# A transformer pair on one core: the order of units and loads in the first stage

## Chip, core and metric

The kernel runs on one core of one Trainium2 chip. The metric is device microseconds of one execution, the median of several. "PE" below is the matrix engine, "ACT" the scalar engine, "DVE" the vector engine; SP issues the loads. Each engine works through its own instructions in the order in which they are written.

## What is computed

Two transformer blocks in float32, 256 tokens of width 2048. The change lies in the front of the first block: a modulation vector from a conditioning vector, a normalised and modulated input for the tokens and for 256 context tokens, and the input projection.

```
mod_l = (jax.nn.silu(c) @ w_ada[l] + b_ada[l])[:, None, :]
mod_c = (jax.nn.silu(c_ctx) @ w_ada[l] + b_ada[l])[None, None, :]
...
h_l = modulate(rms_norm(x, g_mix_norm[l]), sh_a, sc_a)
h_c = modulate(rms_norm(xc, g_mix_norm[l]), csh_a, csc_a)
qa_l, kva_l, kr_l, cb_l, cc_l, ch_l = split_projection(h_l @ w_in[l])
qa_c, kva_c, kr_c, cb_c, cc_c, ch_c = split_projection(h_c @ w_in[l])
```

After it come the key/value and query projections (`wkvk`, `wkvv`, `wqb`), a convolution branch (`wconv`), attention, an output projection (`wout`), a feed-forward part and a second block. Those are not changed, except for where some chunks of `w_ada` are used.

## The kernel before, in words

Weights come from memory in chunks of at most 1 MiB (128 x 2048 floats) through one load queue. A chunk is used in "units". For most weights a unit is split: ACT casts it to a high part `wh` (a 768 or 1024 wide cast, L359) and DVE subtracts to get the low part `wl` (L360). Each product is then three matmuls (`wh` with `XH`, `wl` with `XH`, `wh` with `XL`), all recorded at line 411.

The first stage works over the 16 blocks of 128 channels in eight groups of two. Per group there are

- four "a" units: one 1 MiB chunk of `w_ada` each, not split, eight recorded matmuls `s<-raw,cn`. They accumulate the shift and scale rows of the group.
- then `gen_h`: a copy `arow` on ACT, four "row matmuls" `m<-cst,arow` that turn the rows into columns, small DVE steps (`SHG`), and for the tokens `X`, `XH`, `XL`, for the context `CX`, `cxh`, `cxl`. The context part needs `R0[1]`, the reciprocal root of the context's mean square.
- a "c" unit (18 matmuls), a "q" unit (24, the low-rank query input) and a "k" unit (36, key/value for tokens and context), which need the group's `XH` and `XL`, and k also `cxh` and `cxl`. A "C", "Q" or "K" chunk (0.75, 1 and 0.75 MiB) holds two such units.

The string `FIRST` is the order in which PE takes the units: the n-th "a" is `w_ada` chunk n, four per group, the n-th "c", "q" or "k" is that unit of group n. `LOADS` is the order of the loads. X comes ahead of both strings, the context CX ahead of the first K chunk. An "a" chunk has a ring of four buffers, C, Q and K have one buffer each, so a load waits on the queue until its buffer has been used, and the loads behind it wait too.

`gen_r0(0)` makes the mean square of X, `gen_r0(1)` that of CX: eight squares on ACT, sums on DVE, then matmuls with ones (`m<-sq,ones`): one for X, eight for CX, in pairs of the two token halves. The one for CX runs in one piece after unit c1.

The later chunks of `w_ada` are not used by PE: DVE multiplies each by the conditioning vector and sums (L349). The table `LATE` says behind which chunk of which weight how many of them stand; they go through the same ring of four buffers. The order of all 64 is fixed, and the table moves only the places. Casts are placed ahead of use by `look`, `AHEAD` = 4 units, with `NSPL` = 5 buffers for `wh` and `wl`.

`pump` lets pending pieces of `gen_h` and others go one step further; `kv` calls it after each third of a k unit, `unit_b` not at all.

Of the kernel before, what the change touches and what calls it, by code (L numbers as in the profile page):

```python
# [15 lines left out]
OP = mybir.AluOpType  # L16
# [19 lines left out]
AHEAD0 = 2  # L36
CXB = 3
AHEAD_N = ((0, 0), (0, 2), (1, 0))
FIRST = "aaaacq" "aaaac" "aaakakqc" + 5 * "aaaakqc" + "kq"
LOADS = "aaCaaQ" "aaaaK" + 3 * "aaaaCaaKaaQ"  # L40
NC0 = 2
KVY = 1
MG = (2, 2)
# [4 lines left out]
STAT0 = 0  # L48
ATT = (2, 4)
LATE = {  # L50
    "wconv": {2: 1, 3: 1, 5: 1, 7: 1, 8: 1, 9: 1, 10: 1, 11: 1, 12: 1, 13: 1, 14: 1, 15: 1, 16: 1, 17: 2, 20: 2,
              21: 2, 22: 1, 23: 1, 24: 3},
    "wkvk": {0: 1},
    "wkvv": {0: 1},
    "wqb": {0: 2, 1: 2, 2: 1},
    "wout": {0: 1, 1: 1, 5: 1, 2: 2, 7: 2, 9: 2, 11: 1, 14: 1},
    "wup": {**dict.fromkeys((0, 8, 1, 5, 9, 6), 1), **dict.fromkeys(range(14, 78, 4), 1)},
}
# [151 lines left out]
def _emit(tc, A, out, dbg=None):  # L210
    with ExitStack() as st:
        _body(st, tc, A, out, dbg or {})


def _body(st, tc, A, out, dbg):
    nc = tc.nc
    V, S, TE = nc.vector, nc.scalar, nc.tensor
# [14 lines left out]
    def plan_first():  # L232


        at, of = dict.fromkeys("aCQK", 0), {}
        for n in LOADS:
            i = at[n]
            at[n] += 1
            of[n.lower(), i] = len(chunks)
            if n == "a":  # L240
                chunks.append((A["wada0"][i // 4, i % 4], 2048, None))
            elif n == "Q":
                chunks.append((A["wqa"][i], 2048, "q"))
            else:
                chunks.append((A["wkc"][int(n == "C"), i], 1536, n.lower()))
        at = dict.fromkeys("aqck", 0)
        for n in FIRST:
            i = at[n]
            at[n] += 1
            if n == "a":  # L250
                u = Unit("ada0", of[n, i], (i // 4, i % 4 * 4, 4, 512, 0), True)
                u.native = True
            elif n == "q":
                u = Unit(n, of[n, i // 2], lay["wqa"][i // 2][i % 2], i % 2 == 1)
            else:
                u = Unit(n, of[n, i // 2], (0, 2 * i, 2, 384, 768 * (i % 2)), i % 2 == 1)
            events.append(u)
            first.append((n, i))
        return of
# [17 lines left out]
    of = plan_first()  # L277
# [23 lines left out]
    def pump():  # L301
        for ln in (EV, SIDE, MISC):
            ln.step()
# [13 lines left out]
    extra, pre = [None], {}  # L317

    def done_with(ci):
        raws.pop(ci)  # L320
        while nxt[0] < len(chunks) and room():
            issue()
# [49 lines left out]
    def look(n):  # L372

        seen, j = 0, ep[0]
        while j < len(events) and seen <= n:
            if not isinstance(events[j], tuple):
                seen += 2 if events[j].name in ("wkvk", "wkvv") else 1
            j += 1
        while sp[0] < j and (sp[0] < ep[0] + 1 or not hold(events[sp[0]])):
            split_next()  # L380

    def unit(name, g, n=None):
        while isinstance(events[ep[0]], tuple):
            ep[0] += 1
        u = events[ep[0]]
        mark(u, count[0])
        assert u.name == name and u.g == g, (u.name, u.g, name, g)
        look(ahead[0] if n is None else n)
        ep[0] += 1
        return u  # L390
# [19 lines left out]
    def mm(ps, l, r, start, stop, **kw):  # L410
        count[0] = TE.matmul(ps, l, r, start=start, stop=stop, skip_group_check=True, **kw)  # L411

    def mm3(ps, wh, wl, xh, xl, start, stop):
        mm(ps, wh, xh, start, False)
        mm(ps, wl, xh, False, False)
        mm(ps, wh, xl, False, stop)

    def unit_b(name, g, pst, xh, xl, starts=(0, 2)):

        u = unit(name, g)  # L420
        kt = spec[name][0]
        for n in range(u.w // P):
            for ki in range(u.nk):
                k = u.k0 + ki
                o = ki * u.w + n * P
                mm3(pst(n), u.wh[:, o:o + P], u.wl[:, o:o + P], xh(k, u), xl(k, u),
                    k == 0 and n in starts, k == kt - 1)
        return u.k0 + u.nk >= kt

    def group_b(name, g, xh, xl, hook=None, m=None):  # L430

        m = m or MR.now()
        i = 0
        while True:
            done = unit_b(name, g, lambda n: m.bank(n // 2)[:, n % 2 * T:(n % 2 + 1) * T], xh, xl)
            if hook:
                hook(i)
            i += 1
            if done:
                return m  # L440
            pump()
# [81 lines left out]
    ones = cp.tile([P, P], F32, name="ones")  # L523
# [12 lines left out]
    xh = lambda k, u=None: XH[:, k, :]  # L536
    xl = lambda k, u=None: XL[:, k, :]
# [21 lines left out]
    def rstd(*a):  # L559
        for _ in rstd_steps(*a):  # L560
            pass
# [8 lines left out]
    with tc.tile_pool(name="b0", bufs=1) as b0:  # L570
        extra[0] = b0
        CT = b0.tile([P, 2, KD], F32, name="CT")
        CX = b0.tile([P, KD, T], F32, name="CX")
# [3 lines left out]
        def load_tokens(dst, src):  # L577
            for h in range(4):
                nc.sync.dma_start(dst[:, 4 * h:4 * h + 4, :], A[src][:, 4 * h:4 * h + 4, :])
# [7 lines left out]
        ident = cst("ident")  # L587
        load_tokens(X, "xt")
        pre[of["a", 2]] = lambda: nc.sync.dma_start(VE, A["vecs"])
        pre[of["k", 0]] = lambda: load_tokens(CX, "ctxt")  # L590
        pre[n_first] = load_rest
        while room():
            issue()
# [15 lines left out]
        def gen_r0(w):  # L609

            src = (X, CX)[w]
            ps = m0.t[:, w, :T]
            acc = None
            for q in range(8):
                sq = b0.tile([P, 2, T], F32, name="sq0", tag="sq0", bufs=4)
                S.activation(sq, src[:, 2 * q:2 * q + 2, :], AF.Square)
                if acc is not None:
                    V.tensor_tensor(sq, sq, acc, OP.add)
                acc = sq
                if w and q % 2:  # L620
                    for j in range(2):
                        mm(ps, ones, sq[:, j], q + j == 1, q + j == 8)
                    acc = None
            if not w:
                V.tensor_tensor(acc[:, 0], acc[:, 0], acc[:, 1], OP.add)
                yield
                mm(ps, ones, acc[:, 0], True, True)
            rstd(R0[:, w, :], ps, 1.0 / D, EPS)
            r0_done.add(w)

# [36 lines left out]
        for c in range(4):  # L667
            b = qs[c % 2]
            for k in range(4):
                tr(b.t[:, k * P:(k + 1) * P], CF[:, 0, 4 * c + k:4 * c + k + 1].to_broadcast([P, P]))  # L670
            V.tensor_copy(CBC[:, 512 * c:512 * c + 512], b.t)
        r0 = gen_r0(0)
        next(r0)

        def ada(i):

            g, kc = i // 4, i % 4
            u = unit("ada0", g, 0 if g < 2 else None)
            w = raws[u.chunk]
            for j in range(4):  # L680
                mm(am.t[32 * j:32 * j + 32, :], cn[:, u.k0 + j, :], w[:, j * 512:(j + 1) * 512], kc == 0, kc == 3,
                   tile_position=(0, 32 * j))
            done_with(u.chunk)
            if i == 1:
                next(r0, None)
            if kc == 3:
                EV.add(gen_h(g))
            pump()
            if kc == 3:
                look(0)  # L690
# [3 lines left out]
        def kv():  # L694
            u = unit("k", 0)
            cxh, cxl = CXS[u.k0 // 2]
            for n in range(3):
                for ki in range(2):
                    k = u.k0 + ki
                    o = ki * 384 + n * P  # L700
                    for w, (h, l) in enumerate(((xh(k), xl(k)), (cxh[:, ki, :], cxl[:, ki, :]))):
                        mm3(kvb[n][:, w * T:(w + 1) * T], u.wh[:, o:o + P], u.wl[:, o:o + P],
                            h, l, k == 0 and w == 0, k == KD - 1)
                pump()

        c0 = lambda n: m1.t[:, 1, :T] if n == 2 else cm.t[:, n * T:(n + 1) * T]
        banks = {"q": lambda n: qs[n // 2].t[:, (n % 2) * T:(n % 2 + 1) * T], "c": c0}
        for n, i in first:
            if n == "a":
                ada(i)  # L710
                continue
            while i not in (CXS if n == "k" else XS):
                pump()
            if n == "k":
                kv()
            else:
                unit_b(n, 0, banks[n], xh, xl, (0, 2) if n == "q" else (0,))
                if n + str(i) == "c1":
                    for _ in gen_r0(1):
                        pass  # L720
                pump()
        ahead[0] = AHEAD
        dump("XH", XH.bitcast(F32))
# [14 lines left out]
    with tc.tile_pool(name="b1", bufs=1) as b1:  # L738
# [40 lines left out]
        with tc.tile_pool(name="b1n", bufs=1) as bn:  # L779
# [78 lines left out]
            for g in range(2):  # L858
                u = unit("wkvk", g)
# [9 lines left out]
            for g in range(2):  # L869
                u = unit("wkvv", g)  # L870
# [286 lines left out]
    with tc.tile_pool(name="b2", bufs=1) as b2:  # L1157

        acc = b2.tile([P, 1, 2, T], F32, name="acc2")
# [773 lines left out]
```

## Time and profile before

| | |
|---|---|
| median of 3 runs | 2199.33 us (2196.23 to 2201.58) |
| profiled execution | 2189.7 us |
| its span | 2187.9 us |
| PE busy | 2145.6 us, 98% of the span |
| DVE busy, ACT busy | 1492.4 us (68%), 1100.3 us (50%) |
| loads | 467.71 MB, 214 GB/s on average |

The profiled execution is one run; its own time stands 1.8 us above its span. Busy times overlap between engines. A matmul's recorded duration is longer than the step to the next one, so PE's work is better counted in matmuls per stretch. "PEclk" is the granted clock, 1.00 at 2.4 GHz and 0.50 at 1.2 GHz.

### The profile page before, as it was taken

To read this page: it belongs to the slowest core of one execution; us is meant where nothing else is said; L and a number is where in the kernel's file an instruction comes from. 1 tells how busy PE (TensorE), PEld (TensorE's weight loads), DVE (VectorE), ACT (ScalarE), POOL (GpSimd) and SP (SyncE) were. 2 spreads that over 40 slices of the span, in tenths; PEclk is the share of its full clock that TensorE was granted. 3 is DMA by queue.
4 is the path that set the end of the run, shared out by engine and by line. 5 is a ranking of instruction groups with operands and counts; after the bars stand their busy time and mean duration, and the time that the engine had idled before them with its cause. 6 is when DMAs were issued, how large, how long until landed. Compare 5 with 4: busy or idle time off the path is not lost.

```text
span 2187.9 us, 40079 instructions
## 1 busy us (share of the span) xinstructions
PE 2145.6 (98%) x17282; PEld 2061.5 (94%) x17286; DVE 1492.4 (68%) x1976; ACT 1100.3 (50%) x1500; POOL 0.2 (0%) x4
## 2 busy tenths in 40 slices
PE   6999999999999999999999999999999999999999
PEld 3788889989999999999999989999999999999999
DVE  4458878877876676767777679675666756646565
ACT  3344555445544444455656443445446546645363
POOL 0000000000000000000000000000000000000000
PEclk9999999999999999999999999999999999999999
DMA  9877878858666666645555545444555554445553
GB/s 383 323 286 268 288 244 321 341 219 302 219 231 244 225 239 230 228 162 206 185 188 175 194 154 190 141 152 156 196 174 190 182 191 148 142 173 194 179 175 114
DMA packets 68434, 467.71 MB, mean 214 GB/s; under 512 B 7840, under 2 KB 8352, under 8 KB 16544
## 3 DMA queue, kind: packets, MB, share of 16 engines
q1 hardware_dynamic: 68256, 465.14, 59.0%
q8 instruction: 135, 2.21, 0.4%
q14 instruction: 43, 0.35, 0.0%
HBM read 463.01 MB, written 2.10 MB: 213 GB/s over the span
## 4 chain that ended last, share of the span: by engine, by line
PE 92%; DVE 4%; DMA 3%; ACT 1%; issue 1%; SPq 0%; ACTq 0%; DVEq 0%
PE m L411 78%; PE s L411 13%; DMA rawx<-in_wqa 1%; DVE wl L360 1%; DMA raw<-in_wada 1%; PE s L408 1%; DVE raw L349 1%; ACT wh L359 0%; DMA raw<-in_wconv 0%; DMA X<-in_xt 0%; DVE rp L1306 0%; DVE rp L1307 0%; ACT arow L635 0%; DVE X L1165 0%; DVE rp L788 0%
## 5 line engine op out<-in xcount | busy, mean ns | idle before, releaser
L411 PE MATMUL m<-XH,wh 128*128 128x256 f32 x4032 | 1143.5, 284 | 8.6 <-ACT XH L1206 4.1
L360 DVE TENSOR_TENSOR wl<-raw,wh 128x1024 fp32r<-128x1024 f32 (+1 forms) x672 | 800.3, 1197 | 502.1 <-ACT wh L359 501.2
L411 PE MATMUL m<-XH,wl 128*128 128x256 f32 x4032 | 1132.2, 281 | 0.6 <-DVE wl L360 0.6
L411 PE MATMUL m<-XL,wh 128*128 128x256 f32 x4032 | 1132.2, 281 | 0.1
L359 ACT CAST wh<-raw 128x1024 fp32r<-128x1024 f32 (+1 forms) x672 | 686.7, 1028 | 667.9 <-PE m L411 592.9
L411 PEld LDWEIGHTS m<-XH,wh 128*128 128x128 f32 x4032 | 761.9, 189 | 25.5 <-issue 15.9
L411 PEld LDWEIGHTS m<-XH,wl 128*128 128x128 f32 x4032 | 761.8, 189 | 3.8 <-issue 2.2
L411 PEld LDWEIGHTS m<-XL,wh 128*128 128x128 f32 x4032 | 761.4, 189 | 0.5 <-DVE XL L1209 0.4
L411 PE MATMUL m<-ahl,wh 128*128 128x256 f32 x1376 | 245.0, 281 | 0.5 <-DVE uf L1234 0.5
L411 PEld LDWEIGHTS m<-ahl,wh 128*128 128x128 f32 x1376 | 211.4, 189 | 0.7 <-issue 0.7
L411 PE MATMUL m<-ahl,wl 128*128 128x256 f32 x688 | 193.1, 281 | 0.0
L349 DVE SCALAR_TENSOR_TENSOR raw<-raw,CBC 128x2048 f32<-128x2048 f32 x64 | 145.4, 2283 | 0.5 <-DMA raw<-in_wada 0.4
L411 PEld LDWEIGHTS m<-ahl,wl 128*128 128x128 f32 x688 | 129.7, 189 | 0.0
L411 PE MATMUL s<-XH,wh 128*128 128x256 f32 x416 | 118.0, 284 | 3.5 <-ACT XH L655 3.5
L411 PE MATMUL s<-XL,wh 128*128 128x256 f32 x416 | 117.9, 283 | 0.0
L411 PE MATMUL s<-XH,wl 128*128 128x256 f32 x416 | 117.7, 283 | 0.0
L364 ACT CAST ahl<-AC 128x512 fp32r<-128x512 f32 x88 | 53.8, 611 | 89.0 <-PE m L411 89.0
L365 DVE TENSOR_TENSOR ahl<-AC,ahl 128x512 fp32r<-128x512 f32 x88 | 59.6, 677 | 38.7 <-ACT ahl L364 38.7
L411 PEld LDWEIGHTS s<-XH,wh 128*128 128x128 f32 x416 | 79.4, 191 | 3.7 <-ACT XH L655 3.7
L411 PEld LDWEIGHTS s<-XH,wl 128*128 128x128 f32 x416 | 79.5, 191 | 0.0
L411 PEld LDWEIGHTS s<-XL,wh 128*128 128x128 f32 x416 | 79.4, 191 | 0.0
L360 DVE TENSOR_TENSOR wl<-rawx,wh 128x768 fp32r<-128x768 f32 (+1 forms) x24 | 24.9, 1046 | 61.6 <-ACT wh L359 61.6
(387 smaller groups left out, 1677.6 us busy)
## 6 DMA issues: line engine op xcount, KB each, us to landing
raw<-in_wada SPq DMA_DIRECT2D x96, 1024.0 KB, 6.7
raw<-in_wup SPq DMA_DIRECT2D x86, 1024.0 KB, 4.9
raw<-in_wdown SPq DMA_DIRECT2D x40, 1024.0 KB, 4.8
raw<-in_wpg SPq DMA_DIRECT2D x32, 1024.0 KB, 4.9
raw<-in_wconv SPq DMA_DIRECT2D x28, 768.0 KB, 6.1
raw<-in_wout SPq DMA_DIRECT2D x16, 1024.0 KB, 6.3
raw<-in_wqA SPq DMA_DIRECT2D x16, 1024.0 KB, 4.8
raw<-in_wgA SPq DMA_DIRECT2D x16, 1024.0 KB, 4.8
```

The costliest lines, as they stand in the source:

```text
L349: V.scalar_tensor_tensor(r, r, 1.0, CBC, op0=OP.mult, op1=OP.mult, accum_out=ADA[:, b:b + 1])
L359: S.copy(e.wh[:, :n], r)
L360: V.tensor_tensor(e.wl[:, :n], r, e.wh[:, :n].bitcast(F32), OP.subtract)
L364: S.copy(e.x[:, 0, :e.nk], a)
L365: V.tensor_tensor(e.x[:, 1, :e.nk], a, e.x[:, 0, :e.nk].bitcast(F32), OP.subtract)
L408: count[0] = TE.transpose(o, i, ident)
L411: count[0] = TE.matmul(ps, l, r, start=start, stop=stop, skip_group_check=True, **kw)
```

## The change

The order strings and the late table change, q units let pending work go on after each quarter, and the mean square of CX is summed on DVE and takes one matmul.

```diff
-FIRST = "aaaacq" "aaaac" "aaakakqc" + 5 * "aaaakqc" + "kq"
-LOADS = "aaCaaQ" "aaaaK" + 3 * "aaaaCaaKaaQ"
+FIRST = "aaaac" "aaaaqc" "aaaaqck" + 5 * "aaaakqc" + "kkq"
+LOADS = "aaCaa" "Qaaaa" "aaaaCK" + 2 * "aaaaQaaKaaC" + "aaaaQK"
...
-    "wconv": {2: 1, 3: 1, 5: 1, 7: 1, 8: 1, 9: 1, 10: 1, 11: 1, 12: 1, 13: 1, 14: 1, 15: 1, 16: 1, 17: 2, 20: 2,
+    "wconv": {2: 1, 3: 1, 5: 1, 7: 1, 8: 1, 9: 1, 10: 1, 11: 1, 12: 1, 13: 1, 14: 1, 15: 1, 16: 1, 17: 2, 18: 1, 19: 1, 20: 2,
...
-    "wqb": {0: 2, 1: 2, 2: 1},
+    "wqb": {0: 1, 1: 1, 2: 1},
...
-    def unit_b(name, g, pst, xh, xl, starts=(0, 2)):
+    def unit_b(name, g, pst, xh, xl, starts=(0, 2), tick=None):
...
+            if tick:
+                tick()
...
-        pre[of["k", 0]] = lambda: load_tokens(CX, "ctxt")
+        pre[of["a", 8]] = lambda: load_tokens(CX, "ctxt")
...
-                if w and q % 2:
-                    for j in range(2):
-                        mm(ps, ones, sq[:, j], q + j == 1, q + j == 8)
-                    acc = None
-            if not w:
-                V.tensor_tensor(acc[:, 0], acc[:, 0], acc[:, 1], OP.add)
-                yield
-                mm(ps, ones, acc[:, 0], True, True)
+            V.tensor_tensor(acc[:, 0], acc[:, 0], acc[:, 1], OP.add)
+            yield
+            mm(ps, ones, acc[:, 0], True, True)
...
-        r0 = gen_r0(0)
-        next(r0)
+        sums = [gen_r0(w) for w in range(2)]
+        next(sums[0])
...
-            u = unit("ada0", g, 0 if g < 2 else None)
+            u = unit("ada0", g, 0 if g < 1 else 2 if g < 3 or kc < 3 else 1)
...
-            if i == 1:
-                next(r0, None)
+            if i in (1, 11):
+                next(sums[i > 1], None)
...
-                unit_b(n, 0, banks[n], xh, xl, (0, 2) if n == "q" else (0,))
+                unit_b(n, 0, banks[n], xh, xl, (0, 2) if n == "q" else (0,), pump if n == "q" else None)
                 if n + str(i) == "c1":
-                    for _ in gen_r0(1):
-                        pass
+                    next(sums[1])
```

Three places of the new order follow. In the rows, a tile's number tells buffers apart.

PE from unit c0 (into `s_120` and `m_116`) to unit c1, first before. `s_117` and `s_118` take the q unit, `s_119` the four a units.

```order
L411 MATMUL m_116<-XL_69,wh_206 128x256
L411 MATMUL s_117<-XH_68,wh_224 128x256
...
L411 MATMUL s_118<-XL_69,wh_224 128x256
L411 MATMUL s_119<-raw_170,cn_106 32x512 x4
L411 MATMUL s_119<-raw_176,cn_106 32x512 x4
L411 MATMUL s_119<-raw_190,cn_106 32x512 x4
L411 MATMUL s_119<-raw_196,cn_106 32x512 x4
L411 MATMUL m_116<-cst0_87,arow_294 128x2 x4
L411 MATMUL s_120<-XH_68,wh_296 128x256
```

The same stretch of PE after the change, again from the end of c0 to the start of c1.

```order
L411 MATMUL m_116<-XL_69,wh_200 128x256
L411 MATMUL s_119<-raw_170,cn_106 32x512 x4
L411 MATMUL s_119<-raw_176,cn_106 32x512 x4
L411 MATMUL s_119<-raw_190,cn_106 32x512 x4
L411 MATMUL s_119<-raw_196,cn_106 32x512 x4
L411 MATMUL s_117<-XH_68,wh_252 128x256
...
L411 MATMUL m_116<-cst0_87,arow_276 128x2 x4
...
L411 MATMUL s_118<-XL_69,wh_252 128x256
L411 MATMUL s_120<-XH_68,wh_262 128x256
```

Unit q0 has moved from ahead of the four a units to behind them, and the row matmuls stand inside it, after its first six matmuls. In group 2 q1 stands in the same way around the row matmuls.

ACT from the last square of the context to the copy `arow` of group 2 and a little on, before. `R0` is the reciprocal root; casts from `rawx_202` are k0 and k1, from `rawx_104` q1, from `rawx_300` c2.

```order
L616 ACTIVATE sq0_357<-CX_83 128x512
L549 ACTIVATE R0_114<-rsm_362 128x256
L550 ACTIVATE R0_114<-R0_114 128x256
L655 ACTIVATE cxh_216<-CX_83,SHG_71 128x256 x2
L655 ACTIVATE cxh_308<-CX_83,SHG_71 128x256 x2
L359 CAST wh_387<-rawx_202 128x768
L359 CAST wh_401<-rawx_202 128x768
L359 CAST wh_445<-rawx_104 128x1024
L635 COPY arow_457<-s_119 128x512
L359 CAST wh_459<-rawx_300 128x768
```

The same stretch of ACT after the change; here `rawx_272` is c2 and `rawx_274` k0.

```order
L618 ACTIVATE sq0_354<-CX_83 128x512
L359 CAST wh_370<-rawx_104 128x1024
L359 CAST wh_380<-rawx_272 128x768
L551 ACTIVATE R0_114<-rsm_393 128x256
L552 ACTIVATE R0_114<-R0_114 128x256
L652 ACTIVATE cxh_210<-CX_83,SHG_71 128x256 x2
L652 ACTIVATE cxh_290<-CX_83,SHG_71 128x256 x2
L632 COPY arow_408<-s_119 128x512
L359 CAST wh_410<-rawx_274 128x768
```

The casts of q1 and c2 have moved ahead of the root, those of k0 behind `arow`. In both orders `arow` of group 2 stands behind the root and the four `cxh` copies.

The queue of loads around `wqb`, the difference of the two orders.

```order
 L340 DMA raw<-in_wqb 128x2048
-L340 DMA raw<-in_wada 128x2048 x2
+L340 DMA raw<-in_wada 128x2048
 L340 DMA raw<-in_wqb 128x2048
-L340 DMA raw<-in_wada 128x2048 x2
+L340 DMA raw<-in_wada 128x2048
 L340 DMA raw<-in_wqb 128x2048
```

One late chunk stands behind each of the first two `wqb` chunks where there were two; the two removed ones stand behind `wconv` 18 and 19.

## Rows read from the trace of the kernel before

**Rows 1.** The page, share of the span and chain by engine

```profile
PE 2145.6 (98%) x17282; PEld 2061.5 (94%) x17286; DVE 1492.4 (68%) x1976; ACT 1100.3 (50%) x1500; POOL 0.2 (0%) x4
...
PE 92%; DVE 4%; DMA 3%; ACT 1%; issue 1%; SPq 0%; ACTq 0%; DVEq 0%
```

**Rows 2.** Stretches of 10 us: busy per engine (instructions), PEclk, DMA share, GB/s

```profile
30.00:40.00 10.00, 9.36 (x72) 6.52 (x70) 1.22 (x1) 0.70 (x3) 0.00 (x0) 1.00 1.02 417
...
110.00:120.00 10.00, 8.61 (x73) 8.41 (x72) 8.01 (x14) 5.76 (x9) 0.00 (x0) 1.00 0.91 381
...
210.00:220.00 10.00, 7.30 (x41) 7.10 (x40) 9.13 (x12) 5.45 (x7) 0.00 (x0) 0.67 0.99 366
```

**Rows 3.** Timeline of PE, 35 to 65 us: start, duration, instruction, idle before and releaser

```profile
35.72 3.64 PE L411 MATMUL s<-raw,cn 128*32 128x512 f32 x32
...
43.18 0.58 PE L411 MATMUL s<-XH,wh 128*128 128x256 f32 x1 [2.01 <-ACT XH L655]
...
46.22 0.29 PE L411 MATMUL m<-XH,wl 128*128 128x256 f32 x1
...
57.05 0.58 PE L411 MATMUL m<-XH,wh 128*128 128x256 f32 x1 [3.06 <-ACT wh L359]
...
63.30 0.28 PE L411 MATMUL m<-XH,wh 128*128 128x256 f32 x1
...
64.58 0.28 PE L411 MATMUL m<-cxl,wh 128*128 128x256 f32 x1
```

**Rows 4.** Timeline of ACT, 35 to 320 us

```profile
39.48 0.58 ACT L635 COPY arow<-s 128x512 f32<-128x512 f32 x1 [9.30 <-PE s L411]
...
54.56 1.70 ACT L655 ACTIVATE cxh<-CX,SHG 128x256 fp32r<-128x256 f32 x4 [1.93 <-DVE CX L653]
...
79.79 0.59 ACT L635 COPY arow<-s 128x512 f32<-128x512 f32 x1 [5.43 <-PE s L411]
...
93.64 0.59 ACT L635 COPY arow<-s 128x512 f32<-128x512 f32 x1 [6.17 <-PE s L411]
...
110.24 1.04 ACT L359 CAST wh<-rawx 128x1024 fp32r<-128x1024 f32 x1 [6.61 <-DMA rawx<-in_wqa]
...
140.87 0.58 ACT L635 COPY arow<-s 128x512 f32<-128x512 f32 x1
...
211.28 1.99 ACT L359 CAST wh<-raw 128x1024 fp32r<-128x1024 f32 x2 [8.53 <-DMA raw<-in_wqb]
...
318.09 0.83 ACT L359 CAST wh<-raw 128x768 fp32r<-128x768 f32 x1 [2.19 <-PE m L411]
```

**Rows 5.** Timeline of PE, 110 to 215 us

```profile
111.82 1.05 PE L411 MATMUL m<-cst,arow 128*128 128x2 f32 x8 [1.39 <-ACT arow L635]
...
214.24 0.58 PE L411 MATMUL m<-QAH,wh 128*128 128x256 f32 x1 [2.70 <-ACT QR L888]
```

**Rows 6.** Timeline of the load queue at a8 to a11

```profile
36.85 2.90 SPq L340 DMA_DIRECT2D raw<-in_wada  x4
```

**Rows 7.** Loads issued at 27.0, 204.6 and 307.1 us: size, time to landing

```profile
CX<-in_ctxt SPq DMA_DIRECT2D x1, 512.0 KB, 14.0
...
raw<-in_wqb SPq DMA_DIRECT2D x1, 1024.0 KB, 6.6
...
raw<-in_wconv SPq DMA_DIRECT2D x1, 768.0 KB, 4.3
```

**Rows 8.** Timeline of DVE, 50 to 205 us

```profile
51.31 0.42 DVE L543 TENSOR_SCALAR rsm<-m 128x256 f32<-128x256 f32 x1 [1.22 <-PE m L411]
...
157.66 0.69 DVE L729 COPY X<-s 128x512 f32<-128x512 f32 x1 [0.75 <-PE s L411]
...
198.95 1.23 DVE L360 TENSOR_TENSOR wl<-raw,wh 128x1024 fp32r<-128x1024 f32 x1 [0.69 <-ACT wh L359]
...
202.30 2.29 DVE L349 SCALAR_TENSOR_TENSOR raw<-raw,CBC 128x2048 f32<-128x2048 f32 x1
```

**Rows 9.** One stretch of 1 us: PE busy (matmuls), PEclk, DMA share, GB/s

```profile
219.00:220.00 1.00, 1.00 (x7) 0.50 0.99 420
```

## The prediction

> **What bounds the kernel now.** Read the page first: the matrix engine PE is busy for 98% of the span and holds 92% of the chain that ended last [rows 1]. So a change can pay only where PE stands idle or runs at its lower clock. The stretches of 10 us show where that is. At full speed PE can issue about 86 matmuls in 10 us (one in 0.1165 us, below). From 30 to 40 us it issues 72, although the DMA share is 1.02 at 417 GB/s: the loads set the pace. From 110 to 120 us it issues 73 with the clock at 1.00, and from 210 to 220 us 41 with a mean clock of 0.67 [rows 2]. The change touches both places.
>
> Prices for the first stage come from the timeline of PE [rows 3]. At the full clock 64.58 - 63.30 = 1.28 us hold eleven steps, 0.1165 us each. A c unit (18 matmuls) costs 2.10 us, a q unit (24) 2.80, a k unit (36) 4.19. Four a units back to back take 3.64 us, 0.91 each. A unit's first matmul after a wait lasts 0.58 us instead of 0.28: the lower of the clock's two levels, 1.2 instead of 2.4 GHz. One such start at 43.18 is at full speed again by 46.22, the one at 57.05 only at 63.30; so 3.0 to 6.2 us at half speed, a loss of 1.5 to 3.1 us.
>
> The stage is paced by the copy arow, one per group, which starts when that group's four a units are done [rows 4]. From 79.79 to 93.64 a period is 13.85 us; the sum 4.19 + 2.80 + 2.10 + 3.64 plus row matmuls of 1.05 [rows 5] is 13.8, so PE alone sets that one. The next three periods take 47.23 together, 15.7 each: the cast of a q unit waited 6.61 us for its load (until 110.24) in front of an arow on ACT's in-order queue, and PE idled 1.39 us before the row matmuls at 111.82; there are two such places, in groups 5 and 7 [rows 4, 5].
>
> **The change, part by part.**
>
> *q0 behind group 1.* Before, q0's 2.80 us stand between c0 and a4, and after a7 PE has nothing until XH is ready: arow 39.48, c1 at 43.18 after 2.01 idle, then 3 us at the low clock [rows 3, 4]. After, c0 ends where it does, a4 to a7 run 2.8 us earlier (arow 36.7), and the 3.70 us from arow to XH are covered by q0 with the four row matmuls inside it, 2.80 + 1.05 = 3.85. c1 then runs at full speed from about 40.4 to 42.5 instead of 43.18 to 46.8. Those 4.3 us cannot be cashed at once, because loads come next.
>
> *k0, k1 behind group 2 and the loads so ordered.* The last part of CX lands at 27.0 + 14.0 = 41.0 [rows 7]. Before, a8 was issued at 36.85, after a4's matmuls had freed its buffer, and it came behind chunk K0 [rows 6]. After, a8 to a11 follow CX directly: at 417 GB/s 1 MiB takes 2.5 us, so a11 lands at 50.9, and C1 (0.75 MiB) at 52.8. PE waits for these loads in either kernel, so c1's earlier end is hidden here.
>
> *One sum matmul instead of eight, and what ACT does around it.* The order below shows what is not in the diff: in group 2 arow stands on ACT behind the CX reciprocal root and four cxh copies. The sum matmul comes after a11, and the root on DVE behind c2's low half, which needs C1: 52.8, a cast of 0.83 (as at 318.09, [rows 4]) and about 1 us on DVE, 54.6. From that DVE step to the end of the four cxh copies it took 51.31 to 54.56 + 1.70 = 56.26, that is 4.95 us [rows 4, 8]. So arow of group 2 starts at 59.5 and the row matmuls end at 61.2. PE has only six matmuls of q1 before them and idles about 4 us from 55. This wait takes the place of the old one (57.05, after 3.06 idle). Then follow q1's rest 2.10, c2 2.10, k0 4.19, a12 to a15 3.64: 12.0 us, and 2.2 for the low clock (middle of 1.5 and 3.1). arow of group 3 is at 75.4 instead of 79.79: 4.4 us earlier, but with one k unit (k1, 4.19 us) not yet done. Up to here the change gains 0.2 us.
>
> *From group 3 to the end of the stage.* Before, 79.79 to the last copy of the q banks at 157.66 is 77.87 us [rows 4, 8]. After, k1's 4.19 is added; the casts of q units now stand behind arow, and each Q chunk is issued ahead of the next group's a loads, so the two holes of 1.4 should go: 77.87 + 4.19 - 2.8 = 79.3. The end comes at 75.4 + 79.3 = 154.7: 3.0 us earlier. Bounds: if PE alone sets all four periods, 4 x 13.85 = 55.4 instead of 61.08 - 2.8 = 58.3, and with the smaller clock loss it is 6.6 earlier; if the holes stay and the clock loss is the larger, 0.9 later. I take 3.0, since chunks K1 and K2 still lie between a loads of groups 4 and 6.
>
> *Two 1 MiB ada chunks moved from behind wqb to behind wconv 18 and 19.* wqb's third chunk reuses the buffer of the chunk four places before it. Before, that is an ada chunk which DVE finishes at 202.30 + 2.29 = 204.6; the load, issued then, lands 6.6 us later at 211.2 [rows 7, 8]; ACT waited 8.53 us for it, PE idled 2.70 until 214.24 and was still at 0.50 at 219 to 220 us [rows 4, 5, 9]. After, the place four before is wqb's first chunk, whose second low half ends at 198.95 + 1.23 = 200.2 [rows 8], so the load can land at about 205 and its two casts end near 207; DVE also has two products of 2.29 us fewer ahead of it. PE has work to 211.5, so the hole closes: 2.7 us idle and half of some 6.2 us at the low clock, 5.8 in all. Bounds 0 and 5.8. In their new place the two products cost DVE 2 x 2.29 and the queue 2 x 2.5 us. wconv 20's load took 4.3 us [rows 7], and the first cast of its stretch, at 318.09, had waited 2.19 us for PE, that is for a buffer [rows 4]: casts run four units ahead, 4 x 2.1 = 8 us. I cost it at nothing; without that cover it would be a hole like wqb's, 5.8 us.
>
> **Sum.** 3.0 + 5.8 = 8.8 us earlier. The profiled execution took 2189.7 us (span 2187.9), so 2180.9; the three timed runs have a median of 2199.33, 9.6 above it, and the same difference gives 2190.5.
>
> **The rivals.** *First stage as before, only wqb closes.* The holes before arow go over into late a loads. For it: a DMA share of 0.91 between 110 and 120 us, near its limit [rows 2]. Then 5.8 earlier, 2193.5. *wqb's hole stays* because DVE's split is late by another way: 3.0 earlier, 2196.3. Against it: 4.6 us of DVE work are gone from in front of it. *Both better*: PE alone sets the periods, 12.4 earlier, 2186.9. *The clock.* In this trace the low clock follows the pauses of PE before c1, k0 and wqb's third chunk (2.0 to 3.1 us), but not the pause of 1.39 us, whose ten microseconds stay at 1.00 [rows 2, 3, 5]. If load waits of groups 4 to 7 each grew past that, four starts at 1.5 to 3.1 us would cost about 9: 2199.5, no change.
> The Trainium skill ("TensorE: Matmul & The Clock Gate", section "HAM oscillation — how this bites in real kernels") describes just this, matmul bursts between DMA waits that each start at the low rate, and it speaks against an order that lets PE run ahead of its loads. By that rule group 2 pays, and the trace shows it for two pauses; no row shows it for groups 4 to 7.
>
> *Slower: the moved chunks starve wconv.* wconv 19, 20 and 21 would each come behind one or two more ada chunks in a ring of four buffers. If each became late as wqb was, three holes of 5.8 are 17.4 us, net 8.6 slower: 2207.9. It decides when wconv 20 lands later than 8 us after 318, its cast time plus the lead; before, it landed at about 311.4 (4.3 us after its issue at 307.1, [rows 7]), and two MiB more put it near 317. So it is unlikely.
>
> **How the numbers follow.** Forecast (both parts, 6 to 12 us) 0.60; only wqb 0.15; only the first stage 0.08; better than 12 us 0.05; clock, no change 0.06; slower 0.06. A measurement of this kernel can tell 0.2%, 4.4 us. Faster: 0.60 + 0.05 + most of the 0.15 and a little of the 0.08 = 0.79; same 0.14; slower 0.07. The range takes in the bounds of the two main terms, 2185 to 2198, and leaves out the no-change and slower cases and the far end of the better one.
>
> **What would show it.** Right: arow of group 1 near 36.7 with c1 entered at the full clock; a11's load at 51; arow of group 2 near 59.5 behind four cxh copies with PE idle some 4 us; arow of group 3 near 75; the last q copy near 154.7; no ACT wait for wqb over 3 us, and a clock of 1.00 in the ten microseconds around its third chunk; casts in the wconv stretch waiting for PE, not for loads. Wrong: arow of group 2 after 62, periods above 15 us from group 3 on, or a new DMA wait of ACT at wconv 19 to 21 with PE idle behind it.

## The result, and the profile after

| | before | after |
|---|---|---|
| median of 4 runs each | 2200.45 us (2196.23 to 2202.02) | 2185.34 us (2183.76 to 2186.54) |
| ratio | | 0.9946, 95% interval 0.9925 to 0.9967 |
| profiled execution | 2189.70 us | 2186.54 us |
| arow of groups 1, 2, 3, 7 start at | 39.48, 65.93, 79.79, 140.87 | 37.13, 59.20, 75.53, 131.88 |
| last q copy starts at | 157.66 | 153.63 |
| last QN copy (end of the `wqb` units) starts at | 222.89 | 212.98 |

By the ratio the change is 0.54% faster, 11.9 us of 2200; the ratio is not the quotient of the two medians, which stand 15.1 us apart. The forecast was 2190.5 with a range of 2185 to 2198: the time lies at the range's lower end, 0.3 us inside it. The page of the changed kernel, share of the span and chain by engine, beside [rows 1]:

```profile
PE 2147.1 (98%) x17268; PEld 2061.7 (94%) x17272; DVE 1494.4 (68%) x1980; ACT 1101.9 (50%) x1500; POOL 0.2 (0%) x4
...
PE 94%; DVE 2%; DMA 2%; ACT 1%; issue 0%; SPq 0%; ACTq 0%; DVEq 0%
```

The whole kernel looks the same; what moved is seen in stretches of 10 us, columns as in [rows 2]:

```profile
30.00:40.00 10.00, 10.00 (x69) 6.31 (x69) 2.69 (x6) 1.03 (x3) 0.00 (x0) 0.78 1.02 418
50.00:60.00 10.00, 4.69 (x21) 2.42 (x18) 4.24 (x9) 4.07 (x9) 0.00 (x0) 0.67 1.02 425
60.00:70.00 10.00, 10.00 (x66) 10.00 (x67) 7.19 (x16) 3.05 (x6) 0.00 (x0) 0.75 0.48 199
...
110.00:120.00 10.00, 10.00 (x88) 7.23 (x87) 2.90 (x6) 3.85 (x6) 0.00 (x0) 1.00 1.01 401
200.00:210.00 10.00, 10.00 (x88) 10.00 (x88) 9.97 (x13) 5.94 (x7) 0.00 (x0) 1.00 0.95 338
210.00:220.00 10.00, 10.00 (x70) 8.00 (x69) 9.82 (x13) 3.60 (x5) 0.00 (x0) 1.00 0.59 214
```

Both places of [rows 2] are full: 88 matmuls instead of 73 from 110 to 120 us, and PE never idle at a clock of 1.00 from 200 to 220 us. The third chunk of `wqb` is now cast at 201.19, so it is the stretch from 200 to 210 us, with 88 matmuls, that stands for the one with 41 before. The worst stretch left is 50 to 60 us: PE is busy for 4.69 of 10 us, with the loads at 425 GB/s. The timeline of ACT shows what paces it, beside [rows 4]:

```profile
37.13 0.59 ACT L632 COPY arow<-s 128x512 f32<-128x512 f32 x1 [6.90 <-PE s L411]
...
52.61 0.83 ACT L359 CAST wh<-rawx 128x768 fp32r<-128x768 f32 x1 [6.16 <-DMA rawx<-in_wkc]
54.80 0.42 ACT L551 ACTIVATE R<-rsm 128x256 f32<-128x256 f32 x1 [1.36 <-DVE rsm L545]
...
57.59 1.70 ACT L652 ACTIVATE cxh<-CX,SHG 128x256 fp32r<-128x256 f32 x4 [1.93 <-DVE CX L650]
59.20 0.56 ACT L632 COPY arow<-s 128x512 f32<-128x512 f32 x1
...
75.53 0.59 ACT L632 COPY arow<-s 128x512 f32<-128x512 f32 x1 [8.13 <-PE s L411]
...
89.61 0.59 ACT L632 COPY arow<-s 128x512 f32<-128x512 f32 x1 [6.09 <-PE s L411]
...
131.88 0.59 ACT L632 COPY arow<-s 128x512 f32<-128x512 f32 x1 [6.10 <-PE s L411]
...
201.19 2.01 ACT L359 CAST wh<-raw 128x1024 fp32r<-128x1024 f32 x2 [2.36 <-DMA raw<-in_wqb]
...
212.98 1.02 ACT L884 COPY QN<-m 128x1024 f32<-128x1024 f32 x1 [1.97 <-PE m L411]
```

ACT waits for chunk C1 until 52.61; the root, the `cxh` copies and `arow` follow one behind the other, the last with no idle time of ACT before it. From group 3 on every `arow` waits for PE alone and the periods are 14.1 us ((131.88 - 75.53) / 4 = 14.09). The wait for `wqb` is 2.36 instead of 8.53 us. PE in group 2, beside [rows 3]:

```profile
50.76 1.94 PE L411 MATMUL s<-raw,cn 128*32 128x512 f32 x8 [0.54 <-DMA raw<-in_wada]
52.62 1.22 PE L411 MATMUL m<-sq,ones 128*128 128x256 f32 x2
...
54.71 0.33 PE L411 MATMUL s<-XL,wh 128*128 128x256 f32 x1
59.82 1.87 PE L411 MATMUL m<-cst,arow 128*128 128x2 f32 x8 [4.77 <-ACT arow L632]
...
64.68 0.41 PE L411 MATMUL s<-XL,wh 128*128 128x256 f32 x1
...
65.09 0.28 PE L411 MATMUL s<-XH,wl 128*128 128x256 f32 x1
```

PE stands still for 4.77 us before the row matmuls; the matmuls after it come 0.21 us apart, the lower of the two clock levels, until 64.9. DVE, beside [rows 8], the root's first step and the end of the stage:

```profile
54.35 0.42 DVE L545 TENSOR_SCALAR rsm<-m 128x256 f32<-128x256 f32 x1
...
153.63 0.69 DVE L725 COPY X<-s 128x512 f32<-128x512 f32 x1 [0.72 <-PE s L411]
```

### The profile page after: what moved, and what is told of

It reads as the page before. It is cut to its first block, busy times and chain, and to the rows that moved or that the text cites. A ratio compares the mean times of both kernels' runs of the same rounds, so it can differ in the third digit from the quotient of the medians.

```text
span 2184.8 us, 40059 instructions
## 1 busy us (share of the span) xinstructions
PE 2147.1 (98%) x17268; PEld 2061.7 (94%) x17272; DVE 1494.4 (68%) x1980; ACT 1101.9 (50%) x1500; POOL 0.2 (0%) x4
## 4 chain that ended last, share of the span: by engine, by line
PE 94%; DVE 2%; DMA 2%; ACT 1%; issue 0%; SPq 0%; ACTq 0%; DVEq 0%
PE m L411 80%; PE s L411 14%; DVE wl L360 1%; DMA raw<-in_wada 1%; DMA rawx<-in_wkc 1%; PE s L408 1%; ACT wh L359 0%; DMA X<-in_xt 0%; DVE rp L1302 0%; DVE rp L1303 0%; DVE raw L349 0%; DVE X L1161 0%; ACT cxh L652 0%; DVE uf L1229 0%; DVE uf L1230 0%
```

## The experiments

The theory is the prediction's, in two parts: the first stage and `wqb`. Rivals: that the new order itself changes how closely PE's matmuls follow, since the traces differ in that, and that single steps are worth something else. All kernels with their marks (start in us of the copy `arow` of group 2, of the last q copy and of the last QN copy; matmuls from 500 to 550 us; ratio to the kernel before, on the same chip; e1 to e4 ran on one chip, e5 to e8 on a second, e9 to e12 on a third):

| kernel | arow 2 | q copy | QN copy | matmuls | ratio (95% interval) |
|---|---|---|---|---|---|
| before, shown ahead | 65.93 | 157.66 | 222.89 | 428 | |
| after | 59.20 | 153.63 | 212.98 | 424 | 0.9946 (0.9925 to 0.9967) |
| e1_before_again | 67.88 | 161.11 | 224.21 | 423 | 0.9996 (0.9981 to 1.001) |
| e2_late_only | 67.96 | 160.94 | 220.21 | 428 | 0.9971 (0.9957 to 0.9984) |
| e3_first_stage_only | 59.51 | 154.50 | 217.44 | 424 | 0.9978 (0.9965 to 0.9991) |
| e4_sum_after_a9 | 55.05 | 150.45 | 209.72 | 424 | 0.9931 (0.9913 to 0.9949) |
| e5_no_tick | 58.93 | 155.51 | 214.78 | 423 | 0.9955 (0.9941 to 0.997) |
| e6_q0_back | 58.94 | 153.37 | 212.64 | 424 | 0.9961 (0.9945 to 0.9976) |
| e7_eight_sums | 61.70 | 156.02 | 215.28 | 428 | 0.9967 (0.9954 to 0.998) |
| e8_early_root | 53.79 | 147.82 | 207.09 | 429 | 0.9934 (0.9914 to 0.9953) |
| e9_wconv_doubled | 59.84 | 155.13 | 214.38 | 424 | 0.995 (0.993 to 0.9969) |
| e10_k0_load_first | 61.28 | 155.83 | 215.09 | 424 | 0.9965 (0.9949 to 0.9982) |
| e11_after_again | 59.11 | 154.58 | 213.84 | 423 | 0.9946 (0.9926 to 0.9966) |
| e12_early_root_again | 53.84 | 148.04 | 207.30 | 429 | 0.9907 (0.9886 to 0.9928) |

The two profiles of the changed kernel differ by 0.95 us at the q copy: what lies within 1 us there is not told apart.

**The kernel before, once more** (e1_before_again, no edit).

> The kernel before, unchanged. Its first profile holds 428 matmuls in each 50 us from 500 to 950 us and 424 after that; the changed kernel's holds 423 throughout, so the two profiled spans differ by 3.1 us only while the timed runs differ by 15. Theory A (the pitch belongs to the execution, not to the kernel): this profile shows 423 to 424 matmuls per 50 us from 500 us on, a span of 2196 to 2200, and the same marks in the first 230 us as before: arow of group 3 at 79.8, last q copy at 157.7, last copy to QN at 222.9, each later by up to 1% of the PE-bound part. Rival B (the order of the kernel before gives it the faster pitch): 428 again and a span near 2188. Timed: ratio 1.000, within 0.2%.

The first profile of before had 428 matmuls in 50 us, after 424, both at a granted clock of 1.00 with PE never idle. Stretches of before:

```profile
500.00:550.00 50.00, 50.00 (x428) 50.00 (x427) 36.50 (x45) 28.07 (x36) 0.00 (x0) 1.00 0.76 275
```

Stretches of the same kernel in the new profile, the third one around the pause in group 7, the second around `wqb`:

```profile
500.00:550.00 50.00, 50.00 (x423) 50.00 (x423) 38.53 (x44) 27.45 (x36) 0.00 (x0) 1.00 0.81 301
...
210.00:220.00 10.00, 7.48 (x64) 7.28 (x63) 9.97 (x11) 2.90 (x3) 0.00 (x0) 1.00 0.98 340
...
140.00:150.00 10.00, 8.60 (x59) 8.10 (x56) 5.57 (x11) 5.43 (x9) 0.00 (x0) 0.83 0.90 361
```

PE in that profile, at the same two pauses:

```profile
143.38 1.10 PE L411 MATMUL m<-cst,arow 128*128 128x2 f32 x8 [1.40 <-ACT arow L635]
144.34 0.56 PE L411 MATMUL m<-XH,wh 128*128 128x256 f32 x1
...
217.51 0.38 PE L411 MATMUL m<-QAH,wh 128*128 128x256 f32 x1 [2.52 <-ACT QR L888]
```

So the distance of the steps differs between executions of the same code, 428 and 423. Whether a kernel's order makes the closer steps more likely is not shown. The same pauses also had other consequences. After the 1.40 us pause of group 7 the clock now fell (matmuls of 0.41 us until 147.3; 59 in the stretch), where the first profile stayed at 1.00 with 73. It also fell after the 1.31 us pause of group 5 (0.83 from 110 to 120 us, there too 1.00 in the first). After the pause at `wqb` it now stayed at 1.00, where it had been at 0.50 [rows 9]. The first stage ended at 161.11 instead of 157.66, more than the 1% that was expected. Of these 3.45 us 1.95 were there at `arow` of group 2 already (67.88 after 65.93), ahead of both pauses; the other 1.5 came behind them. The part from the q copy to the QN copy took 63.10 instead of 65.23 us.

**Each half alone.** e2_late_only is the kernel before with this part of the change:

```diff
-... 16: 1, 17: 2, 20: 2,
+... 16: 1, 17: 2, 18: 1, 19: 1, 20: 2,
-    "wqb": {0: 2, 1: 2, 2: 1},
+    "wqb": {0: 1, 1: 1, 2: 1},
```

> The kernel before with the late table of the change alone. Theory A (the two parts add, each as read from the marks): first stage as before (last q copy at 157.7), ACT's wait for wqb's third chunk falls from 8.5 to under 3 us, PE does not idle there, the last copy to QN comes 5.9 us earlier (217.0), and the time falls by 5.8, ratio 0.9974. Rival C (the moved products of DVE are paid for at wconv 18 to 21): the mark at QN is 5.9 earlier but the time falls by 0 to 3, with a DMA or DVE wait and PE idle near 300 to 330 us.

e3_first_stage_only is the changed kernel with the same lines put back.

> The changed kernel with the late table of before: the first stage alone. Theory A: arow of group 2 at 59.2, of group 3 at 75.5, last q copy at 153.6, the wqb hole as before (ACT waits about 8.5 us, PE idles about 2.7 and runs at the low clock), the last copy to QN at 218.9, time 4.0 to 5.5 lower (the 4.0 of the marks and up to 1.5 of pitch), ratio 0.9975 to 0.9982. Rival D (an earlier first stage shrinks the wqb hole by itself, or deepens it): the distance from the last q copy to the last QN copy differs from 65.2 by more than 1 us.

The two waits of ACT for `wqb`, first with the table moved, then without:

```profile
209.15 2.00 ACT L359 CAST wh<-raw 128x1024 fp32r<-128x1024 f32 x2 [3.11 <-DMA raw<-in_wqb]
```

```profile
208.29 1.99 ACT L359 CAST wh<-raw 128x1024 fp32r<-128x1024 f32 x2 [8.66 <-DMA raw<-in_wqb]
```

PE and the clock of e3_first_stage_only at that place (timeline, then the stretch):

```profile
211.25 0.39 PE L411 MATMUL m<-QAH,wh 128*128 128x256 f32 x1 [2.84 <-ACT QR L884]
```

```profile
210.00:220.00 10.00, 8.76 (x69) 8.28 (x70) 9.66 (x14) 6.05 (x8) 0.00 (x0) 1.00 0.88 328
```

The q copy of e2_late_only lies at 160.94, as in e1_before_again and not at 157.7, so its gain is read from there on. From the q copy to the QN copy it is 59.27 with the table moved and 62.94 without (after: 59.35, 59.26 in its second profile). The 62.94 is the sign of rival D, but the unchanged kernel had 63.10 in its second profile, so no effect of the earlier first stage is needed for it. The move closes the hole and is worth 3.6 to 3.8 us against kernels whose clock stayed up there, 5.9 against the first profile of before. The first stage alone ends 6.6 before e1_before_again's. The two gains at the QN copy against that kernel, 4.00 and 6.77, add to 10.8; the whole change has 11.2 and 10.4. In the times, 0.29% and 0.22% add to 0.51%, beside the change's 0.54%; each is known to some 0.13% only, the change to 0.21%.

**The root earlier.** e4_sum_after_a9 is the changed kernel with the sum of CX after a9:

```diff
-            if i in (1, 11):
+            if i in (1, 9):
```

> The changed kernel, but the context's sum matmul and its root come after a9 instead of a11, so that the chain in front of arow of group 2 runs while PE waits for a10 and a11; the cast of q1 then stands behind it. Theory A (arow of group 2 is held by the chain sum, root, cxh on ACT's in-order queue, and PE sets the pace from there): arow of group 2 at 55.5 to 56.5 instead of 59.2, row matmuls end about 58.5 instead of 61.7, last q copy 2 to 4 earlier than 153.6. Rival E (the loads set the pace of groups 3 to 7): arow of group 2 comes earlier, but the last q copy moves by less than 0.7.

PE and ACT of that kernel in group 2:

```profile
54.47 0.48 PE L411 MATMUL s<-XH,wh 128*128 128x256 f32 x1 [2.50 <-ACT wh L359]
55.72 0.58 PE L411 MATMUL s<-XH,wl 128*128 128x256 f32 x1 [0.78 <-DVE wl L360]
```

```profile
53.39 1.76 ACT L359 CAST wh<-rawx 128x1024 fp32r<-128x1024 f32 x2
55.05 0.57 ACT L632 COPY arow<-s 128x512 f32<-128x512 f32 x1
```

The wait for the root is gone, 3 to 4 us earlier at the q copy; what is late next is the cast of q1, now behind the `cxh` copies on ACT. e8_early_root therefore also takes the casts of group 2 a unit earlier:

```diff
-            u = unit("ada0", g, 0 if g < 1 else 2 if g < 3 or kc < 3 else 1)
+            u = unit("ada0", g, 0 if g < 1 else (2, 3, 2, 1)[kc] if g == 2 else 2 if g < 3 or kc < 3 else 1)
-            if i in (1, 11):
+            if i in (1, 9):
```

> e4 with two casts moved: q1's ahead of the root, c2's behind arow, so that arow of group 2 stands only behind the cxh copies and q1's first matmuls are ready when a11 is done. Theory A: arow of group 2 at 53 to 54 (e4: 55.05, changed kernel: 59.2), PE idles under 1 us before the row matmuls, so the low clock ends sooner as well; last q copy 1.5 to 4 earlier than e4's 150.45, time 0.1 to 0.2% under e4. Rival E (the loads of a16 on become the bound once PE is this early): arow of group 2 at 53.5 but the last q copy within 0.7 of e4's, with PE waiting for a loads in groups 4 to 7.

PE of that kernel in group 2:

```profile
47.92 0.91 PE L411 MATMUL m<-sq,ones 128*128 128x256 f32 x2 [1.17 <-DVE sq L622]
...
54.41 1.26 PE L411 MATMUL m<-cst,arow 128*128 128x2 f32 x8 [1.31 <-ACT arow L632]
```

The pause before the row matmuls shrinks from 4.77 to 1.31 us, where under 1 was expected, and the q copy is 5.8 earlier than in after and 2.6 earlier than in e4_sum_after_a9. The time does not show that second step: the ratios are 0.9934 and 0.9931. The kernel was run again beside the changed kernel on one chip.

> The kernel with the reciprocal root two a units earlier and the casts of group 2 one unit earlier, once more, on the same chip as the changed kernel. Theory A (group 2's wait for the root is the largest loss left in the first stage): 4 to 7 us faster than the changed kernel on this chip, ratio to the kernel before 0.991 to 0.994, arow of group 2 at 53.5 to 54.5, last q copy 147 to 149. Rival (the difference seen was one between chips and executions): within 2 us of the changed kernel.

> The changed kernel once more, for a comparison on the same chip with the other kernels of this call. Theory A (its profiled execution gains 9 to 10 us by last QN copy over the first profile of the kernel before, and the rest of the timed difference is the closer steps of that profile): ratio to the kernel before 0.994 to 0.996, last q copy 152.5 to 154.5, last QN copy 212 to 214, about 423 or 428 matmuls in 50 us. Rival (part of the gain comes after the QN mark): ratio as before but QN mark to end shorter than 1972 us at 423 matmuls in 50 us.

The q copy is 6.5 earlier than in the second profile of after, the medians are 2174.92 and 2185.20 us: 10.3 us where 4 to 7 were expected, and the stage explains 6.5 of them. Both profiles of e8's kernel had 428 to 429 matmuls in 50 us and both of after 423 to 424, so the rest may lie in the steps, as between the two profiles of before; that is not shown for the timed runs, and whether this kernel draws the close steps more often, two profiles can't tell. On that chip the kernel beats both others.

**q units without ticks** (e5_no_tick: pending work doesn't go on inside a q unit).

```diff
-                unit_b(n, 0, banks[n], xh, xl, (0, 2) if n == "q" else (0,), pump if n == "q" else None)
+                unit_b(n, 0, banks[n], xh, xl, (0, 2) if n == "q" else (0,), None)
```

> The changed kernel without the pump after each quarter of a q unit, so that the row matmuls of groups 1 and 2 come after q0 and q1 instead of inside them. Theory A: in group 1 the row matmuls end 2.1 us later, c1 waits about 2 us for XH, and this is hidden by the loads of a8 to a11 (arow of group 2 within 0.7 us of 59.2). In group 2 q1 is done before arow, so the wait for arow is shorter but c2 then waits for XH with nothing in between: arow of group 3 and the last q copy (153.6) 0.5 to 2.5 later, time 0 to 0.1% more than the changed kernel's. Rival F (the row matmuls inside the q unit are what the first stage gains by): last q copy 4 or more later, back at 157 to 158.

```profile
41.94 0.39 PE L411 MATMUL s<-XH,wh 128*128 128x256 f32 x1 [1.52 <-ACT XH L652]
...
64.19 0.58 PE L411 MATMUL s<-XH,wh 128*128 128x256 f32 x1 [3.32 <-ACT XH L652]
```

The timeline of PE shows c1 and c2 waiting for `XH`, which in after q0 and q1 cover; it costs 0.9 to 1.9 us at the q copy, the lower end of which can't be told from nothing, and too little for the times to show.

**q0 back in its old place** (e6_q0_back).

```diff
-FIRST = "aaaac" "aaaaqc" "aaaaqck" + 5 * "aaaakqc" + "kkq"
+FIRST = "aaaacq" "aaaac" "aaaaqck" + 5 * "aaaakqc" + "kkq"
```

> The changed kernel with q0 put back between c0 and a4 (group 0 as before the change), all else as changed. Theory A (until group 2 the loads set the pace, so q0's new place gains nothing by itself): arow of group 1 at 39.5 to 40.5 instead of 37.1, c1 waits for XH at the low clock, but a11 still comes at 50.8 and arow of group 2 at 59.2, last q copy within 0.7 us of 153.6. Rival G (every microsecond PE saves in group 1 is kept): last q copy 2.8 to 4.3 later, 156.5 to 158.

```profile
40.11 1.05 PE L411 MATMUL m<-cst,arow 128*128 128x2 f32 x8 [0.76 <-ACT arow L632]
42.68 0.39 PE L411 MATMUL s<-XH,wh 128*128 128x256 f32 x1 [1.52 <-ACT XH L652]
```

The pauses of group 1 are back on PE, and the marks of group 2 and of the end are where they were: the loads of a8 to a11 hide them.

**Eight sum matmuls again** (e7_eight_sums: the one sum is multiplied eight times, with the scale divided by eight).

```diff
-            mm(ps, ones, acc[:, 0], True, True)
-            rstd(R0[:, w, :], ps, 1.0 / D, EPS)
+            m = 8 if w else 1
+            for r in range(m):
+                mm(ps, ones, acc[:, 0], r == 0, r == m - 1)
+            rstd(R0[:, w, :], ps, 1.0 / (m * D), EPS)
```

> The changed kernel with the context's sum matmul done eight times over (the same operand added up eight times and the scale divided by eight), so that PE does as many of them as before the change, in one piece behind a11. Theory A (this matmul stands on the chain to arow of group 2): each costs 0.5 us at the full and up to 1 us at the low clock, less 1.6 us that DVE spends on c2's low half in any case: arow of group 2 at 61.5 to 64.5 instead of 59.2, the last q copy 2 to 5 later than 153.6. Rival E (loads pace groups 3 to 7): last q copy within 0.7.

```profile
52.51 4.28 PE L411 MATMUL m<-sq,ones 128*128 128x256 f32 x16
```

In the recorded timeline of PE they take 4.28 instead of 1.22 us, in front of the root; `arow` of group 2 is 2.5 later, the q copy 1.4 to 2.4. This is the price of eight in one piece behind a11; before the change they stood behind c1, from 46.81 us on, ahead of the a units of group 2.

**K0 loaded ahead of the context again** (e10_k0_load_first).

```diff
-LOADS = "aaCaa" "Qaaaa" "aaaaCK" + 2 * "aaaaQaaKaaC" + "aaaaQK"
+LOADS = "aaCaa" "Qaaaa" "KaaaaC" + 2 * "aaaaQaaKaaC" + "aaaaQK"
```

> The changed kernel with one edit of the loads undone: chunk K0 (0.75 MiB) loaded again ahead of the context and a8, instead of behind a11. C1 stays behind a11. Theory A (loads set the pace up to the root, and the root stands behind the cast of C1, which lands in sum at the same time in either order since K0 now comes ahead of it): a11 and C1 land about 1.9 us later (0.75 MiB at 417 GB/s), copy arow of group 2 at 60.5 to 61.5 instead of 59.2, last q copy 1 to 2 us later, 154.5 to 156. Theory B (the place of K0 does not matter, the matmul order alone sets group 2): arow of group 2 at 59 to 59.6 and the last q copy within 0.4 us of 153.6. Theory C (K0 late was what made group 3 wait): arow of group 3 earlier than 75.0.

```profile
54.69 0.83 ACT L359 CAST wh<-rawx 128x768 fp32r<-128x768 f32 x1 [8.93 <-DMA rawx<-in_wkc]
...
61.28 0.56 ACT L632 COPY arow<-s 128x512 f32<-128x512 f32 x1
```

C1's cast and `arow` both come 2.1 us later: the loads carry the root, by way of ACT's order. The q copy is 1.3 to 2.2 later.

**Twice as many chunks behind wconv 18 and 19** (e9_wconv_doubled).

```diff
-... 18: 1, 19: 1, 20: 2, 21: 2, 22: 1, 23: 1, 24: 3},
+... 18: 2, 19: 2, 20: 2, 21: 2, 22: 1, 23: 1, 24: 1},
```

> The changed kernel with twice as many late ada chunks behind wconv 18 and 19 (two each instead of one, taken from behind wconv 24). Theory A (the prediction's zero: casts there run ahead of PE and the queue has room): last q copy 153 to 155 and last QN copy 212 to 214 as in the changed kernel, the casts in the wconv stretch still wait for PE and not for a load, PE has no pause of over 1 us between 290 and 345 us, time within 0.2% of the changed kernel. Theory B (starved wconv): the two added MiB make the load of wconv 20 or 21 late, a wait of ACT for wconv of over 2 us with PE idle behind it, up to 5.8 us for each hole, 0.2 to 0.6% slower than the changed kernel.

ACT, then PE, of that kernel:

```profile
315.35 0.84 ACT L359 CAST wh<-raw 128x768 fp32r<-128x768 f32 x1 [5.67 <-DMA raw<-in_wconv]
...
325.33 0.83 ACT L359 CAST wh<-raw 128x768 fp32r<-128x768 f32 x1 [6.98 <-DMA raw<-in_wconv]
```

```profile
330.44 0.66 PE L408 MATMUL s<-cst,w 128*128 128x128 f32 x4 [2.71 <-ACT w L926]
```

The trace is the rival's, the time is the theory's: casts wait for loads, PE pauses for 2.71 us, and the ratio is that of the changed kernel. From the QN copy to the second cast `XH` (L1001) behind the `wconv` units it takes 152.8 us, against 148.6 and 150.2 in the two profiles of after and 148.1 and 151.1 in those of before. So one chunk each costs nothing that shows, and two are past the cover. What they cost, 1.7 to 4.7 us by these five profiles, is of the size of the ratio's interval, 0.2% or 4 us, so the time can neither show nor exclude it.

## Why the prediction was right, and where its sizes were off

**q0 and group 1: right.** `arow` at 37.13 (36.7 forecast); c1 entered with matmuls of 0.28 us; and nothing of it could be cashed, as e6_q0_back shows.

**Loads and the root in group 2: right.** a11's matmuls start at 50.76 (load forecast for 50.9), C1's cast at 52.61 (52.8), DVE's root step at 54.35 (54.6), `arow` at 59.20 (59.5), idle 4.77 (4), `arow` of group 3 at 75.53 (75.4). That this wait takes the place of the old one was the step that kept the forecast small, and e4_sum_after_a9 and e8_early_root show that it is worth 3.2 to 6.8 us. The one sum matmul, not priced by itself, spares 1.4 to 2.4 us against eight at the same place.

**Group 3 to the end: undersized.** Forecast 79.3, measured 153.63 - 75.53 = 78.1, so 4.0 instead of 3.0 earlier against the same profile. The prediction counted two holes of 1.4 us. The trace of before has a third, in front of an a unit of group 5. It stands here with the hole of group 7, from the timeline of PE (the hole of 1.39 is in [rows 5]):

```profile
107.75 1.07 PE L411 MATMUL s<-raw,cn 128*32 128x512 f32 x8 [1.21 <-DMA raw<-in_wada]
...
141.50 1.05 PE L411 MATMUL m<-cst,arow 128*128 128x2 f32 x8 [1.40 <-ACT arow L635]
```

The three are 1.21 + 1.39 + 1.40 = 4.0 us, and with k1's 4.19 added the stretch became 77.87 + 4.19 - 78.1 = 4.0 shorter. The changed kernel has no pause of PE left from 60 to 150 us, so the chunks K1 and K2 between the a loads made no new holes.

Against e1_before_again, where the pauses of groups 5 and 7 brought the low clock, the q copy is 6.5 to 7.5 earlier, and this stretch, k1 added, 5.3 to 5.5 shorter with pauses of 1.31 and 1.40 only. The prediction held from one execution that 1.4 us don't lower the clock; a second one showed that they can, so there closing those two holes was worth more than their idle time.

**`wqb`: right here, too large in general.** Against the profile that it was read from, 65.23 - 59.35 = 5.9 (5.8 forecast). The half of it that was the clock isn't paid in every execution: 3.6 to 3.8 against e1_before_again and e3_first_stage_only.

The Trainium skill ("TensorE: Matmul & The Clock Gate", section "HAM oscillation — how this bites in real kernels"), weighed as the clock rival, has matmul bursts behind DMA waits start at the low rate each time. The trace agrees for group 2, where PE stood still for 4.77 us (though for ACT), and groups 4 to 7 had no pause left. For the 1.4 us pauses of groups 5 and 7 and for the one of 2.5 to 2.8 us at `wqb` the profiles of before and of e3_first_stage_only show both outcomes.

**`wconv` at nothing: right in the time, not in its sign.** In the first profile of after no cast waits for a `wconv` load between 285 and 345 us, as in the two of before. In other kernels with the moved table they do, as in e2_late_only (timeline of ACT, 285 to 370 us):

```profile
323.97 0.83 ACT L359 CAST wh<-raw 128x768 fp32r<-128x768 f32 x1 [4.60 <-DMA raw<-in_wconv]
```

The longest such wait is 6.02 us in e4_sum_after_a9 and 1.52 in e11_after_again; e3_first_stage_only, without the move, has none over 0.4. The three kernels with the move have no pause of PE of 1 us between 285 and 345 us, so the lead of the casts covered these waits; e9_wconv_doubled shows that the cover is nearly used up.

**The sum: right,** though the two terms share it differently from execution to execution. (Two slips change nothing: 41.0 + 4 x 2.5 is 51.0 and not 50.9, and the worse bound of the first stage comes to 0.7 us later and not 0.9.) At the QN copy 9.9 us earlier than in the same profile (8.8 forecast), 10.4 and 11.2 than in e1_before_again; the ratio gives 7.3 to 16.5. e11_after_again repeats the ratio at 0.9946, and its 1975.9 us from QN copy to the end of the span are no shorter than the 1973.7 of e1_before_again: nothing was gained behind `wqb`.

**The base: the step that missed.** The sum was taken from a profiled execution 9.6 us below the median, and the same difference was added back. So the forecast of the time is the median of three runs less 8.8 us, and the one of the profile is that execution less 8.8; they missed in opposite directions.

The profile came out at 2186.5 instead of 2180.9, since the first profile of before had the closer steps: 428 instead of 424 matmuls from 500 to 550 us, as again from 900 to 950. From the QN copy to the end of its span it took 1965.0 us, the second profile of before 1973.7, the profile of after 1971.8: it gained 9.9 us up to the QN copy and lost 6.8 behind it.

The time came out at 2185.3 instead of 2190.5, and there the base stood high. The kernel before has medians of 2195.33, 2193.58 and 2194.46 us in the three later series, each on one chip (29, 27 and 17 runs), against 2199.33 for the three runs of the forecast; less 8.8 they give 2184.8 to 2186.5. The changed kernel has 2185.34 and, in e11_after_again, 2185.20, there 9.3 below the kernel before. Whether the chip of the first runs made them longer, or so few fell high by chance, is not shown.

## What to carry to other kernels

Before a stage is priced from one profile, a second profile of the same kernel tells which of its losses repeat: most of the idle time did here (the pause of 1.21 us in group 5 did not), what the clock added to it did not. The base of a forecast wants more runs than three: here it stood 4 to 6 us above the later medians, half of the gain. When a copy that PE needs stands in an in-order queue, list what stands ahead of it there; moving the root two units ahead and a cast one gave 5.6 to 6.8 us at the end of the stage, beside the 9.9 to 11.2 us of the whole change at the QN copy.

## What the runs showed that was not expected

At a granted clock of 1.00, with PE never idle, the same code ran 428 matmuls of 128x256 in 50 us in one execution and 423 in another, 0.1168 and 0.1182 us each. A pause of 1.40 us left the clock at 1.00 in one profile of the kernel before and was followed by 0.83 in the mean of its 10 us in another; a pause of 2.70 us was followed by 0.50 for some 6 us, while pauses of 2.52 us (the same kernel) and 2.84 us (e3_first_stage_only) at the same place left it at 1.00.
